# A two-layer hybrid decoder trunk on one core: the mixers' weight subtractions move from VectorE to GpSimd, and weights get four staging tiles instead of two

## The chip, the cores and the metric

The kernel runs on one core of a Trainium2 chip. The metric is the device time of one execution in microseconds (us); the median of three runs before the change is 2559.37 us (2557.65 to 2565.87).

Engine names are those of the profile: PE is TensorE's matmul, PEld its weight load, DVE is VectorE, ACT is ScalarE, POOL is GpSimd, SP is SyncE, which here only issues transfers. L94 is line 94 of the kernel.

## The reference

Input x is 1024 tokens by 1024 columns, fp32, and two layers are applied to it. Each layer is a mixer and an MLP, both with a norm ahead and a norm behind, added to x:

```python
h = rms_norm(x, g_pre_mix)
z = h @ w_in                      # 1024 x 2568: columns for three head groups
out_m = sigmoid(mo) * rms_norm(mlstm_chunkwise(...))       # 4 heads, chunks of 128
out_s = sliding_window_gqa(rope(sq), rope(sk), sv, sinks)  # 8 heads, window 128
out_d = rms_norm(differential_attention(rope(dq), rope(dk), dv, lam)) * (1 - lam_init)
x = x + rms_norm(concat([out_m, out_s, out_d]) @ w_out, g_post_mix)
h2 = rms_norm(x, g_pre_mlp)
x = x + rms_norm(square(relu(h2 @ w_up)) @ w_down, g_post_mlp)
```

All of it is fp32.

## The kernel before, in words

**Products in three parts.** Every large matmul is made from two parts of each operand. The high part (hi) is the fp32 value cast to the shorter type float32r, the low part (lo) is the value minus its high part. A product is then hi x hi + hi x lo + lo x hi, three matmuls in a row. For 128 rows of contraction the order is (weight hi, data hi), (weight hi, data lo), (weight lo, data hi), so a tile's first low part is read by its third matmul (in the combined projection of natural layout, by its second).

**Weights.** `load_w` (L103) brings a weight tile into SBUF in pieces of 512 columns (392 for the packing w_g). For each piece it takes a staging tile from the pool `raw` (tile rw), lets SP issue the transfer (L109), lets ACT cast it to the high part, and lets DVE subtract that from the staging tile, which gives the low part. Without a gain this is `split`:

```python
def split(hi, lo, src):
    nc.scalar.copy(hi, src)                              # L93
    nc.vector.tensor_sub(lo, src, hi.bitcast(F32))       # L94
```

The staging tile is free again when cast and subtraction are done; the next transfer into it waits for that on SP. `raw` has two tiles, 2 KB per partition each. The rest of the kernel uses `split` for activations too, so L93 and L94 appear with many tiles. The packings of w_in and the groups that load them are: w_t (13 tiles of 128x1024 per layer: differential q and k, sliding-window q and k, mLSTM q and k; `proj_tiles`, tile wt, matmuls L285), w_v (mLSTM values and output gate; `nat_group`, tile wv), and w_g (gates and the values of the other two; `p_g2`, tile wg). w_g of layer 0 has its own staging and does not go through `load_w`. w_out is loaded in `out_group` (tiles wo, or woh and wol). w_up (with a gain, L116 and L117, DVE) and w_down (tiles wdh and wdl) belong to the MLP.

**Order of the work.** The program is written as layer by layer: projections, differential attention (`e_diff`, four software-pipelined steps per pair of query blocks), the other projections, then sliding-window attention and mLSTM side by side, then the output projection in two groups of contraction tiles with the norms and transposes for the MLP, then the MLP in eight chunks of up and down. A scheduler with priorities orders the instructions on each engine when the program is built. `ahead(n)` raises the priority of what it encloses; weight loads have `ahead(1000)`. So the projections' matmuls fill PE while the attention waits, and weight transfers, casts and subtractions stand among the attention's instructions on SP, ACT and DVE. Each engine then runs its own list strictly in that order.

**What Pool did.** Pool computes the inverse roots of the norms (`rstd_of`, L153, tile rs, a power of -0.5), in differential attention a product with the softmax's reciprocal (L545, same tile), and some memsets (L672, L731 to L736). Nothing of the weights ran on it.

**Names in the profile.** rot, t and tab belong to the rotary embedding; d_rope, s_ropeq, s_ropek, m_qk, m_rows, mix_d and x_mid are DRAM tensors by which the stages hand on their results; ks, qs, kk and qq are attention operands read back from them. e is a tile of attention scores (L496 to L506), yc and z the mLSTM convolution (L683), h2T, hT and lT the transposed activations.

Of the kernel before, what the change touches and what calls it, by code (L numbers as in the profile page):

```python
# [10 lines left out]
F32 = mybir.dt.float32  # L11
# [6 lines left out]
P = 128  # L18
# [16 lines left out]
def hybrid_kernel(ctx: ExitStack, tc: tile.TileContext, x_in, w_t, w_g, w_v, w_out, w_up, w_down,  # L35
                  pb, cv, gains, g_mlp, rope_t, masks, out):
    nc = tc.nc
# [9 lines left out]
    def pool(tag, bufs, space=None):  # L47
        kw = {} if space is None else {"space": space}
        pools[tag] = ctx.enter_context(tc.tile_pool(name="p_" + tag, bufs=bufs, **kw))
# [6 lines left out]
    pool("at", 2)  # L56
    pool("pt", 2)
    pool("ev", 6)
    pool("raw", 2)
    pool("od", 3)  # L60
    pool("ys", 1)
    pool("mo", 1)
# [10 lines left out]
    def new(tag, shape, name, dt=F32):  # L73
        return pools[tag].tile(list(shape), dt, name=name, tag=tag)
# [10 lines left out]
    def PS(tag, name):  # L85
        return new(tag, (P, 512), name)

    def ahead(n):

        return tc.high_priority(offset=n) if n else nullcontext()  # L90
# [4 lines that stand above are left out]
# [5 lines left out]
        nc.scalar.copy(hi, raw)  # L100
        nc.vector.tensor_sub(lo, raw, hi.bitcast(F32))

    def load_w(hi, lo, src, step, gain=None):  # L103


        for c in range(0, hi.shape[1], step):
            with ahead(1000):
                r = new("raw", (P, step), "rw")
                nc.sync.dma_start(r, src[:, c:c + step])  # L109
            with ahead(1000):  # L110
                if gain is None:
                    split(hi[:, c:c + step], lo[:, c:c + step], r)
                    continue
                for j in range(step // P):
                    cs, rj, g = slice(c + j * P, c + j * P + P), r[:, j * P:j * P + P], gain[:, c // P + j:c // P + j + 1]
                    nc.scalar.activation(hi[:, cs], rj, AF.Copy, scale=g)  # L116
                    nc.vector.scalar_tensor_tensor(out=lo[:, cs], in0=rj, scalar=g, in1=hi[:, cs].bitcast(F32),  # L117
                                                   op0=ALU.mult, op1=ALU.subtract)
# [84 lines left out]
    for j in range(4):  # L203
        if j == 1:
            load_x(1)
        r = new("wd", (P, 2, 392), "wg0")
# [11 lines left out]
    for l in range(DEPTH):  # L218
# [37 lines left out]
        def proj_tiles(*groups):  # L256


            wts = []
            for idx, _, _, _, wtag in groups:  # L260
                for i in idx:
                    if wtag == "whl":
                        w = new("whl", (P, 2, 1024), "wt", F32R)
                        hi, lo = w[:, 0], w[:, 1]
                    else:
                        hi, lo = (new(wt_, (P, 1024), "wt", F32R) for wt_ in wtag)
                    load_w(hi, lo, w_t[l, i], 512)
                    wts.append((hi, lo))
            for half in range(2):
                wi = iter(wts)  # L270
                for idx, evac, tables, rtag, _ in groups:
                    if tables is not None:
                        with ahead(1000):
                            tab = new(rtag[1], (P, 2, 512), "tab")
                            nc.sync.dma_start(tab, rope_t[tables, :, :, half * 512:(half + 1) * 512])
                    qs = []
                    for i in idx:
                        hi, lo = next(wi)
                        q = PS("mm", "pt")
                        n = 0  # L280
                        for k in range(8):
                            kc = slice(k * P, (k + 1) * P)
                            for a, b in ((hi[:, kc], hT[half][:, :, kc]), (hi[:, kc], lT[half][:, :, kc]),
                                         (lo[:, kc], hT[half][:, :, kc])):
                                nc.tensor.matmul(q, lhsT=a, rhs=b, start=n == 0, stop=n == 23)  # L285
                                n += 1
                        qs.append(q)
                        if tables is None:
                            with ahead(1000):
                                evac(i, half, q)  # L290
                    if tables is not None:
                        with ahead(1000):
                            evac(half, qs, tab, rtag[0])
# [55 lines left out]
        def nat_mm(q, t, w_of, n):  # L349
            i = 0  # L350
            for k in range(8):
                lh = hT[t // 4][:, t % 4, k * P:(k + 1) * P]
                ll = lT[t // 4][:, t % 4, k * P:(k + 1) * P]
                wh, wl = w_of(k)
                for a, b in ((lh, wh), (lh, wl), (ll, wh)):
                    nc.tensor.matmul(q[:, 0:n], lhsT=a, rhs=b, start=i == 0, stop=i == 23)  # L356
                    i += 1
# [335 lines left out]
        def nat_group(idx, evac):  # L693
            wv = []
            for j in range(2):
                w = new("whl", (P, 2, 1024), "wv", F32R)
                load_w(w[:, 0], w[:, 1], w_v[l, idx, :, 1024 * j:1024 * j + 1024], 512)
                wv.append(w.rearrange("p s (k c) -> p s k c", k=4))
            for t in range(NT):
                q = PS("mm", "pn")  # L700
                nat_mm(q, t, lambda k: (wv[k // 4][:, 0, k % 4], wv[k // 4][:, 1, k % 4]), 256)
                with ahead(1000):
                    evac(t, q[:, 0:256])
# [118 lines left out]
        def out_group(k0, slots, first, fin):  # L822
            wo = []
            nk = 4
            for k in range(nk):
                if slots[k] == "whl":
                    w = new("whl", (P, 2, DM), "wo", F32R)
                    hi, lo = w[:, 0], w[:, 1]
                else:
                    hi = new(slots[k], (P, DM), "woh", F32R)  # L830
                    lo = new(slots[k], (P, DM), "wol", F32R)
                kt = mix_kt[k0 + k]
                load_w(hi, lo, w_out[l, kt * P:(kt + 1) * P, :], 512)
                wo.append((hi, lo))
            for t in range(NT):
                ts = slice(t * P, (t + 1) * P)
                mx = mxs[k0 // 4, t]
                with ahead(EARLY):
                    if k0 == 0:
                        load_split(mx[:, 0, 0:2], mx[:, 1, 0:2], mix_d[:, :, ts].rearrange("k p n -> p k n"))  # L840
                    else:
                        split(mx[:, 0, 2:4], mx[:, 1, 2:4], mst["out"][:, :, ts])
                for n in range(2):
                    q = PS("mm", "po")
                    i = 0
                    for k in range(nk):
                        for a, b in ((0, 0), (0, 1), (1, 0)):
                            nc.tensor.matmul(q, lhsT=mx[:, a, k], rhs=wo[k][b][:, n * 512:(n + 1) * 512],  # L848
                                             start=i == 0, stop=i == 3 * nk - 1)
                            i += 1  # L850
                    a = acc[t // 4][:, t % 4, n * 512:(n + 1) * 512]
                    with ahead(EARLY):
                        if first:
                            nc.scalar.copy(a, q)
                        else:
                            nc.vector.tensor_add(a, a, q)  # L856
                if fin is not None:
                    with ahead(1000):
                        fin(t)
# [75 lines left out]
        def p_g2():  # L935
            for k in range(8):
                if k < 4:
                    w = new("ws", (P, 2, 392), "wg", F32R)
                else:
                    if k % 2 == 0:  # L940
                        w2 = new("whl", (P, 2, 2, 392), "wg", F32R)
                    w = w2[:, k % 2]
                if l == 0:
                    split(w[:, 0], w[:, 1], wg0[k // 2][:, k % 2])
                else:
                    load_w(w[:, 0], w[:, 1], w_g[l, :, k, :], 392)
                wg.append(w)
            for t in range(NT):
                if l == 0 and t + 1 < NT:
                    first_norm(t + 1)  # L950
                g2(t)
            gating()
# [10 lines left out]
        def p_g1():  # L963
            nat_group(0, mv_evac)
            nat_group(1, mo_evac)
# [58 lines left out]
        for c in range(len(ffs)):  # L1024
# [4 lines left out]
            for f in range(nf):  # L1029
                w = new("whl", (P, 2, 1024), "wu", F32R)  # L1030
# [9 lines left out]
            for f in range(nf):  # L1040
                r0 = ffs[c][f] * P
                hi = new("wd", (P, DM), "wdh", F32R)
                lo = new("ws", (P, DM), "wdl", F32R)
# [60 lines left out]
            for j, (t, n) in enumerate(groups[4:]):  # L1104
                q = PS(ptag[j % 4], "pd")
                i = 0
                for f in range(nf):
                    i = down_mm(q, t, n, f, i)
# [93 lines left out]
```

## Time and profile before

| | |
|---|---|
| median of 3 runs | 2559.37 us |
| the profiled execution | 2563.38 us, its span 2561.6 us |
| mean granted TensorE clock | 0.972 |
| busy PE, DVE, ACT, Pool | 2397.5, 1457.8, 1076.1, 90.8 us |
| mixer of layer 0, MLP of layer 0 | about 0 to 593 us, 593 to 1250 us |
| mixer of layer 1, MLP of layer 1 | about 1250 to 1867 us, 1867 to 2561.6 us |

The span runs from the first to the last instruction of the program. Rows of groups read: line, engine, operation, output tile <- input tiles, shape, count, then busy us and mean ns of one, then the engine's idle time just before them and what ended most of it. The chain of waits is followed back from the last instruction: at each step to what released it, or else to the instruction before it on its engine. A piece of it that is a transfer means that nothing but that transfer was awaited there. "issue" is time in which an engine waited for nothing that the profile shows. Rows of waits read: who waited <- for whom: us in total, times, longest us.

### The profile page before, as it was taken

To read this page: it belongs to the slowest core of one execution; us is meant where nothing else is said; L and a number is where in the kernel's file an instruction comes from. 1 tells how busy PE (TensorE), PEld (TensorE's weight loads), DVE (VectorE), ACT (ScalarE), POOL (GpSimd) and SP (SyncE) were. 2 spreads that over 40 slices of the span, in tenths; PEclk is the share of its full clock that TensorE was granted. 3 is DMA by queue.
4 is the path that set the end of the run, shared out by engine and by line. 5 is a ranking of instruction groups with operands and counts; after the bars stand their busy time and mean duration, and the time that the engine had idled before them with its cause. 6 is when DMAs were issued, how large, how long until landed. Compare 5 with 4: busy or idle time off the path is not lost.

```text
span 2561.6 us, 32491 instructions
## 1 busy us (share of the span) xinstructions
PE 2397.5 (94%) x11556; PEld 1991.8 (78%) x11556; DVE 1457.8 (57%) x3604; ACT 1076.1 (42%) x2657; POOL 90.8 (4%) x174
## 2 busy tenths in 40 slices
PE   8888989889999999999999998878899999999998
PEld 7767867667888888888778777867678888888887
DVE  6676888775234434443675876867742344334436
ACT  4244777656313312331433645756553123213312
POOL 0000000010000000000000000000100000000000
PEclk9998999999999999999999989989999999999999
DMA  5444354333012101110442334433321112112204
GB/s 169 146 141 132 92 125 121 100 103 107 25 41 66 59 24 50 66 50 25 173 163 86 117 126 132 137 87 106 113 90 41 34 58 66 32 36 66 66 22 160
DMA packets 146002, 227.42 MB, mean 89 GB/s; under 512 B 22512, under 2 KB 60592, under 8 KB 145840
## 3 DMA queue, kind: packets, MB, share of 16 engines
q1 hardware_dynamic: 143680, 221.70, 28.1%
q10 hardware_dynamic: 2160, 3.65, 0.4%
q8 instruction: 91, 1.49, 0.2%
q14 instruction: 71, 0.58, 0.1%
HBM read 179.09 MB, written 46.20 MB: 88 GB/s over the span
## 4 chain that ended last, share of the span: by engine, by line
PE 73%; DMA 11%; DVE 7%; ACT 4%; issue 2%; POOL 1%; SPq 1%; DVEq 0%; POOLq 0%; ACTq 0%
PE pu L1012 26%; PE pd L1057 25%; PE pt L285 7%; PE po L848 2%; PE pg L356 2%; PE pn L356 2%; POOL rs L153 1%; DMA mb<-m_rows 1%; DMA qs<-d_rope 1%; PE pv L528 1%; DMA mix_d<-oo 1%; PE sp L493 1%; DMA mxl<-mix_d 1%; DMA rw<-in_w_t_dram 1%; PE ss L611 1%
## 5 line engine op out<-in xcount | busy, mean ns | idle before, releaser
L1012 PE MATMUL pu<-h2T,wu 128*128 128x512 f32 x3072 | 703.6, 390 | 0.1
L1012 PEld LDWEIGHTS pu<-h2T,wu 128*128 128x128 f32 x3072 | 577.4, 188 | 121.2 <-DVE h2T L94 1.1
L1057 PE MATMUL pd<-wdh,u 128*128 128x512 f32 x2048 | 635.2, 390 | 1.1 <-DVE acm L1068 1.1
L1057 PEld LDWEIGHTS pd<-wdh,u 128*128 128x128 f32 x2048 | 384.8, 188 | 81.1 <-DVE acm L1068 1.5
L1057 PE MATMUL pd<-wdl,u 128*128 128x512 f32 x1024 | 399.0, 390 | 0.0
L1068 DVE TENSOR_TENSOR acm<-acm,pd 128x512 f32<-128x512 f32 x224 | 153.1, 686 | 309.1 <-PE pd L1057 309.0
L1015 ACT ACTIVATE r<-pu 128x512 f32<-128x512 f32 x128 | 75.2, 588 | 537.9 <-PE pu L1012 537.9
L285 PE MATMUL pt<-hT,wt 128*128 128x512 f32 x832 | 287.2, 411 | 2.7 <-DVE lamp L228 1.5
L116 ACT ACTIVATE wu<-rw,gk 128x128 fp32r<-128x128 f32 x512 | 160.2, 390 | 184.7 <-PE pu L1012 132.3
L117 DVE SCALAR_TENSOR_TENSOR wu<-rw,gk,wu 128x128 fp32r<-128x128 f32 x512 | 154.2, 351 | 140.9 <-ACT wu L116 140.8
L1057 PEld LDWEIGHTS pd<-wdl,u 128*128 128x128 f32 x1024 | 192.6, 188 | 39.8
L1018 DVE TENSOR_TENSOR r<-r 128x512 f32<-128x512 f32 x128 | 88.4, 690 | 222.5 <-ACT u L1017 222.5
L285 PEld LDWEIGHTS pt<-hT,wt 128*128 128x128 f32 x832 | 160.5, 196 | 33.6 <-issue 2.3
L285 PE MATMUL pt<-lT,wt 128*128 128x512 f32 x416 | 170.2, 409 | 0.0
L153 POOL TENSOR_TENSOR rs<-ms,mhalf 128x1 f32<-128x1 f32 (+2 forms) x112 | 78.9, 709 | 2351.8 <-DVE ms L151 2283.2
L94 DVE TENSOR_TENSOR wdl<-rw,wdh 128x512 fp32r<-128x512 f32 x128 | 88.5, 692 | 105.1 <-ACT wdh L93 105.0
L848 PE MATMUL po<-woh,mxl 128*128 128x512 f32 x384 | 135.1, 410 | 10.4 <-DVE acc L856 7.8
L93 ACT CAST wdh<-rw 128x512 fp32r<-128x512 f32 x128 | 79.3, 620 | 129.2 <-DMA rw<-in_w_down_dram 129.2
L499 ACT ACTIVATE e<-e,nb 128x256 f32<-128x256 f32 (+7 forms) x128 | 99.4, 777 | 52.4 <-DVE nb L496 47.1
L493 PE MATMUL sp<-ks,qs 96*128 96x512 f32 (+2 forms) x192 | 74.0, 396 | 41.0 <-DMA qs<-d_rope 17.0
L356 PE MATMUL pn<-wv,hT 128*128 128x256 f32 x512 | 110.0, 296 | 0.2 <-ACT mv L707 0.2
L496 DVE CUSTOM_DVE_ANT_0 e<-sp,mdif 128x512 f32<-128x512 f32 (+3 forms) x128 | 74.5, 585 | 33.1 <-PE sp L493 24.0
(225 smaller groups left out, 3361.0 us busy)
## 6 DMA issues: line engine op xcount, KB each, us to landing
rw<-in_w_up_dram SPq DMA_DIRECT2D x128, 256.0 KB
rw<-in_w_down_dram SPq DMA_DIRECT2D x128, 256.0 KB
rw<-in_w_t_dram SPq DMA_DIRECT2D x52, 256.0 KB
tab<-in_rope_dram SPq DMA_DIRECT2D x20, 512.0 KB
xt<-in_x_dram SPq DMA_DIRECT2D x16, 512.0 KB
d_rope<-rot SPq DMA_DIRECT2D x32, 256.0 KB
s_ropeq<-rot SPq DMA_DIRECT2D x32, 256.0 KB
qq<-s_ropeq SPq DMA_DIRECT2D x16, 512.0 KB
```

What stands on the lines that cost most here:

```text
L94: nc.vector.tensor_sub(lo, src, hi.bitcast(F32))
L116: nc.scalar.activation(hi[:, cs], rj, AF.Copy, scale=g)
L117: nc.vector.scalar_tensor_tensor(out=lo[:, cs], in0=rj, scalar=g, in1=hi[:, cs].bitcast(F32), op0=ALU.mult, op1=ALU.subtract)
L153: nc.gpsimd.tensor_tensor(out=rs, in0=ms, in1=mhalf[:, 0:n], op=ALU.pow)
L285: nc.tensor.matmul(q, lhsT=a, rhs=b, start=n == 0, stop=n == 23)
L356: nc.tensor.matmul(q[:, 0:n], lhsT=a, rhs=b, start=i == 0, stop=i == 23)
L493: nc.tensor.matmul(sp[:, 0:w], lhsT=qs[0:96, m, (q % 4) * P:(q % 4 + 1) * P], rhs=ks[m][0:96, c0:c0 + w], start=True, stop=True)
L499: nc.scalar.activation(e[:, 0:L], e[:, 0:L], AF.Exp, bias=nb[:, nch - 1:nch], scale=-1.0, accum_out=den[:, m:m + 1])
L848: nc.tensor.matmul(q, lhsT=mx[:, a, k], rhs=wo[k][b][:, n * 512:(n + 1) * 512], start=i == 0, stop=i == 3 * nk - 1)
L1012: nc.tensor.matmul(q, lhsT=w[:, a, kc], rhs=h2[b + half][:, :, kc], start=n == 0, stop=n == 23)
L1057: nc.tensor.matmul(q, lhsT=U[f][a][:, t * P:(t + 1) * P], rhs=D[f][b][:, n * 512:(n + 1) * 512], start=i == 0, stop=i == 3 * nf - 1)
L1068: nc.vector.tensor_add(a, a, q)
```

## The change

The pool `raw` gets four tiles instead of two. `load_w` gets an argument that names the engine of the subtraction; for all packings of w_in and for w_out it is Pool, for w_down it stays DVE. w_up, which has a gain, keeps its path on ACT and DVE. The staging pool serves all of them.

```diff
-    pool("raw", 2)
+    pool("raw", 4)
...
-    def load_w(hi, lo, src, step, gain=None):
+    def load_w(hi, lo, src, step, gain=None, low=None):
...
                 if gain is None:
-                    split(hi[:, c:c + step], lo[:, c:c + step], r)
+                    nc.scalar.copy(hi[:, c:c + step], r)
+                    (low or nc.vector).tensor_sub(lo[:, c:c + step], r, hi[:, c:c + step].bitcast(F32))
                     continue
...
-                    load_w(hi, lo, w_t[l, i], 512)
+                    load_w(hi, lo, w_t[l, i], 512, low=nc.gpsimd)
...
-                load_w(w[:, 0], w[:, 1], w_v[l, idx, :, 1024 * j:1024 * j + 1024], 512)
+                load_w(w[:, 0], w[:, 1], w_v[l, idx, :, 1024 * j:1024 * j + 1024], 512, low=nc.gpsimd)
...
-                load_w(hi, lo, w_out[l, kt * P:(kt + 1) * P, :], 512)
+                load_w(hi, lo, w_out[l, kt * P:(kt + 1) * P, :], 512, low=nc.gpsimd)
...
-                    load_w(w[:, 0], w[:, 1], w_g[l, :, k, :], 392)
+                    load_w(w[:, 0], w[:, 1], w_g[l, :, k, :], 392, low=nc.gpsimd)
```

In the changed kernel the cast of a weight without a gain is L112 and its subtraction L113; every line behind them has a number that is one higher than before (rs is L154 and L546, the stores of rot are L319).

The scheduler makes new lists from this. On SP, at the start of layer 1's mixer, where the rotated q and k (rot) are stored to d_rope and read back as ks and qs, and the packing w_g is loaded into rw, the list before is:

```order
L318 DMA d_rope_11179<-rot 8x16x512 x2
L452 DMA ks<-d_rope_11179 32x2x512
L453 DMA ks<-d_rope_11179 64x2x512
L464 DMA qs<-d_rope_11178 64x2x512
L318 DMA d_rope_11178<-rot 8x16x512 x2
L465 DMA qs<-d_rope_11178 32x2x512
L318 DMA d_rope_11178<-rot 8x16x512 x2
L109 DMA rw<-in_w_g_dram 128x392 x3
L318 DMA d_rope_11179<-rot 8x16x512 x2
L109 DMA rw<-in_w_g_dram 128x392
L109 DMA rw<-in_w_t_dram 128x512
```

The same place on SP in the changed kernel:

```order
L276 DMA tab<-in_rope_dram 128x2x512
L319 DMA d_rope_11179<-rot 8x16x512 x2
L109 DMA rw<-in_w_g_dram 128x392 x2
L453 DMA ks<-d_rope_11179 32x2x512
L454 DMA ks<-d_rope_11179 64x2x512
L465 DMA qs<-d_rope_11178 64x2x512
L319 DMA d_rope_11178<-rot 8x16x512 x2
L466 DMA qs<-d_rope_11178 32x2x512
L319 DMA d_rope_11178<-rot 8x16x512 x2
L109 DMA rw<-in_w_t_dram 128x512 x4
```

Before, the last four of the eight w_g loads stand behind the first ks and qs loads and behind stores of rot. Now the last two stand ahead of them, the other six further up, and the next four loads of w_t come where three loads of w_g were.

On Pool, from the end of layer 0's differential attention to the start of layer 1 (rs of 128x4 is mLSTM's, rs of 128x1 that of the norms on whole rows, x32 of them in layer 0 and at its border), the list before is:

```order
L545 TENSOR_TENSOR rs<-rs,rd 128x2
L153 TENSOR_TENSOR rs<-ms,mhalf 128x4 x8
L153 TENSOR_TENSOR rs<-ms,mhalf 128x1 x32
L672 MEMSET z 128x3 x2
L153 TENSOR_TENSOR rs<-ms,mhalf 128x2
L545 TENSOR_TENSOR rs<-rs,rd 128x2
```

The same place on Pool in the changed kernel; mb is a buffer of the mLSTM, wo and wol are w_out, wt the first tiles of layer 1's w_t:

```order
L737 MEMSET mb_3889 128x2x2
L113 TENSOR_TENSOR wo<-rw,wo 128x512 x4
L113 TENSOR_TENSOR wol<-rw,woh 128x512 x4
L154 TENSOR_TENSOR rs<-ms,mhalf 128x4 x7
L113 TENSOR_TENSOR wol<-rw,woh 128x512 x4
L154 TENSOR_TENSOR rs<-ms,mhalf 128x4
L113 TENSOR_TENSOR wol<-rw,woh 128x512 x4
L154 TENSOR_TENSOR rs<-ms,mhalf 128x1 x16
L113 TENSOR_TENSOR wt<-rw,wt 128x512 x4
L154 TENSOR_TENSOR rs<-ms,mhalf 128x1 x11
L113 TENSOR_TENSOR wt<-rw,wt 128x512 x4
```

Before, nothing stood between these inverse roots. Now subtractions of weights stand ahead of the mLSTM's first rs, between its last ones, ahead of the norms of the output projection, and twice among the norms at the border of the layers. In differential attention they stand among the pairs of rs in the same way, mostly two at a time. In the whole list of Pool there are 108 of them, and at 29 places a run of them is followed by an rs. PE's own list in the mixers is reordered too, since the scheduler picks other projection matmuls between the attention's.

## The prediction

> **What bounds the kernel now.** I read the head of the page first, then the busy time by stage, then the chain of waits.
>
> ```profile
> span 2561.6 us, 32491 instructions
> PE 2397.5 (94%) x11556; PEld 1991.8 (78%) x11556; DVE 1457.8 (57%) x3604; ACT 1076.1 (42%) x2657; POOL 90.8 (4%) x174
> PE 73%; DMA 11%; DVE 7%; ACT 4%; issue 2%; POOL 1%; SPq 1%; DVEq 0%; POOLq 0%; ACTq 0%
> ```
>
> TensorE (PE) is busy for 94% of the span, and Pool is almost empty. The view of busy time by stretches, cut at the borders of the mixers and MLPs of the two layers, shows where the other 6% lie. A row is a stretch and its length, then busy us and instruction counts of PE, PEld, DVE, ACT and POOL, the granted clock, the DMA share and GB/s.
>
> ```profile
> 0.00:593.00 593.00, 511.72 (x2754) 427.28 (x2754) 429.26 (x1220) 336.12 (x867) 41.05 (x81) 0.95 0.43 126
> 593.00:1250.00 657.00, 655.78 (x2886) 542.13 (x2886) 271.90 (x536) 196.18 (x452) 0.00 (x0) 1.00 0.17 56
> 1250.00:1867.00 617.00, 543.00 (x2896) 454.17 (x2894) 455.88 (x1266) 341.11 (x878) 45.01 (x85) 0.94 0.40 120
> 1867.00:2561.60 694.60, 687.01 (x3026) 568.21 (x3024) 300.81 (x585) 202.69 (x463) 4.74 (x8) 1.00 0.18 60
> ```
>
> In the MLP stretches (rows 2 and 4) PE idles for 1.2 and 7.6 us. Nothing that concerns staging can be won there. In the mixer stretches (rows 1 and 3, together 1210 us) PE idles for 81.3 + 74.0 = 155.3 us, and DVE is busy for 429.3 + 455.9 = 885.2 us, 73%. So the change can act on those 155 us, and on them alone. The chain of waits says what ends last there; its summary by line and its long pieces:
>
> ```profile
> by line: PE pu L1012 25.6%; PE pd L1057 24.9%; PE pt L285 7.2%; PE po L848 2.5%; PE pg L356 2.4%; issue 2.0%; PE pn L356 1.9%; POOL rs L153 1.3%; DMA mb<-m_rows 1.3%; DMA qs<-d_rope 1.3%; PE pv L528 1.2%; DMA mix_d<-oo 1.2%; PE sp L493 1.2%
> ...
> 98.99 6.41 DMA rw<-in_w_t_dram
> ...
> 378.69 4.77 DMA rw<-in_w_out_dram
> ...
> 514.77 9.10 DMA rw<-in_w_up_dram
> ...
> 671.31 43.52 PE pu L1012 x192
> ...
> 1341.87 5.75 DMA rw<-in_w_g_dram
> ...
> 1785.73 7.95 DMA rw<-in_w_up_dram
> ```
>
> In the MLP the chain is unbroken PE (one piece of 43.52 us after another). In the mixers it hops between engines and transfers, and weight landings (tile rw) are among its pieces.
>
> **Part 1: four staging tiles instead of two.** A weight load is issued on SP when its rw buffer is free, that is when the low part two loads earlier has been subtracted. With four buffers it need only be four loads back, so the load of the next weight tile no longer follows the subtraction of this one. The order shows SP's loads standing earlier: in the stretch ahead of 1341.87 us above, the last w_g loads stood behind the ks and qs loads and several d_rope stores, and now stand ahead of them. What that is worth at most is PE's idle time inside these pieces of the chain, from the view by stretches with their borders:
>
> ```profile
> 98.99:105.40 6.41, 3.51 (x17) 2.60 (x15) 0.47 (x1) 0.00 (x0) 0.00 (x0) 0.94 0.64 205
> 378.69:383.46 4.77, 3.17 (x15) 1.62 (x13) 3.87 (x15) 4.73 (x14) 0.00 (x0) 1.00 0.91 267
> 514.77:523.87 9.10, 6.58 (x29) 5.07 (x27) 2.73 (x9) 0.42 (x1) 1.01 (x1) 1.00 0.37 101
> 1341.87:1347.62 5.75, 2.00 (x11) 1.62 (x9) 0.00 (x0) 0.00 (x0) 0.00 (x0) 0.95 0.50 166
> 1785.73:1793.68 7.95, 6.50 (x26) 4.72 (x26) 3.45 (x7) 2.38 (x5) 0.00 (x0) 1.00 0.36 104
> ```
>
> PE idles for 33.98 - 21.77 = 12.2 us in them. I take all of it, **-12.2 us**; the lower bound is nothing, if the next wait (mostly another transfer, as the chain's DMA share of 11% suggests) is just as late. In the MLP the deeper staging costs nothing, since PE's own work covers every load.
>
> **Part 2: subtractions leave DVE.** These are the groups of weight subtractions on DVE (count, then busy us, mean ns, idle time before and its cause):
>
> ```profile
> L94 DVE TENSOR_TENSOR wt<-rw,wt 128x512 fp32r<-128x512 f32 x52 | 34.9, 685 | 31.0 <-ACT wt L93 30.7
> L94 DVE TENSOR_TENSOR wol<-rw,woh 128x512 fp32r<-128x512 f32 x24 | 16.0, 687 | 3.2 <-ACT woh L93 2.1 <-PE ss L611 0.9
> L94 DVE TENSOR_TENSOR wv<-rw,wv 128x512 fp32r<-128x512 f32 x16 | 10.4, 684 | 0.0
> L94 DVE TENSOR_TENSOR wo<-rw,wo 128x512 fp32r<-128x512 f32 x8 | 5.4, 684 | 0.4 <-issue 0.3
> L94 DVE TENSOR_TENSOR wg<-rw,wg 128x392 fp32r<-128x392 f32 x8 | 4.4, 562 | 13.5 <-ACT wg L93 13.5
> ```
>
> That is 108 instructions and 34.9 + 16.0 + 10.4 + 5.4 + 4.4 = 71.1 us. DVE's part of the chain is 7% of 2561.6, 179 us, nearly all of it in the mixers, or 179/885.2 = 20% of DVE's busy time there. If the 71.1 us lie on the chain as often as the rest, they are worth 71.1 x 0.20 = **-14.3 us**. The rows also show 30.7 + 13.5 + 2.1 = 46.3 us in which DVE stood behind a copy on ACT that had not come; that blocking goes to Pool too. At the same 20% it would be another 9.3 us; I keep it for the low end only, since much of it is the same late landing as in part 1.
>
> **Part 3: what Pool takes for one.** No row shows a wide subtraction on Pool. The nearest:
>
> ```profile
> L545 POOL TENSOR_TENSOR rs<-rs,rd x32: 194/195/812, 145.2 to 1653.6; 128x2 f32<-128x2 f32 x32
> L734 POOL MEMSET mb<- 64x256 f32 x8 | 2.4, 305 | 0.3
> L736 POOL MEMSET mb<- 128x4 f32 x4 | 0.4, 109 | 0.2
> ```
>
> A two-input instruction with almost no elements takes 0.195 us (the middle one of min/median/max), and a written element costs (305 - 109)/252 = 0.78 ns, 0.40 us for 512. If both reads and the write run side by side, one takes 0.6 us; one after the other, 0.195 + 3 x 0.40 = 1.4 us. I take 1.2, nearer the upper end, because no row shows Pool overlapping them. 108 of them keep Pool busy for 130 us, 11% of the 1210 us, which it has. A page of the Trainium skill, GPSIMD Engine Reference, section 3.1, gives 4497 ns for 2048 fp32 elements of this kind; a quarter of that would be an estimate of 1.12 us, and the terms below would shrink by a few tenths.
>
> Each low part is ready 1.2 - 0.69 = 0.51 us later. A tile's third matmul reads it, but weights come ahead of use: of the 108, few were awaited.
>
> ```profile
> PEld sp L493 <- DVE wt L94: 4.9, 1, 4.9
> ```
>
> That is the longest such wait. I charge 8 cases, **+4 us** (bounds 0 and 108 x 0.51 = 55 us).
>
> **Part 4: Pool and DVE in each other's way.** The timeline shows, of Pool and then of DVE, one multiplication of two elements that took 0.64 instead of 0.195 us. It ended 0.06 us after a DVE instruction with both inputs in SBUF:
>
> ```profile
> 284.55 0.64 POOL L545 TENSOR_TENSOR rs<-rs,rd 128x2 f32<-128x2 f32 x1
> ```
> ```profile
> 283.85 1.28 DVE L506 SCALAR_TENSOR_TENSOR e<-e,r 128x1024 f32<-128x1024 f32 x1
> ```
>
> So DVE can hold Pool up. The reverse, Pool holding up DVE, no row shows, as no Pool instruction reads long. If it does, the victims are instructions like these:
>
> ```profile
> L506 DVE SCALAR_TENSOR_TENSOR e<-e,r 128x128 f32<-128x128 f32 (+3 forms) x64 | 51.9, 811 | 0.6
> L683 DVE SCALAR_TENSOR_TENSOR yc<-z,cvt,yc 128x512 f32<-128x512 f32 x48 | 35.8, 746 | 1.7 <-ACT yc L677 1.1 <-issue 0.2
> ```
>
> These two groups have 112 instructions; with the smaller groups of the kind I reckon about 300. Each meets a running subtraction in 11% of cases and waits half of 1.2 us: 300 x 0.11 x 0.6 = 20 us, at 20% on the chain **+4 us** (bounds 0, and the rival below). The Trainium skill, SBUF — State Buffer, section "Who interferes with whom", states that a DVE instruction with two SBUF inputs contends with a Pool instruction that reads SBUF, and that the second to issue fully blocks. The trace agrees for the one direction (0.64 us against 0.195).
>
> **Part 5: what is queued behind them on Pool.** Pool is in order, and its inverse roots (rs, L153, then a product, L545) now stand behind subtractions that themselves wait for ACT and a landing. In the order, a run of subtractions stands just ahead of an rs at 29 places. The first row here gives rs its mean:
>
> ```profile
> L153 POOL TENSOR_TENSOR rs<-ms,mhalf 128x1 f32<-128x1 f32 (+2 forms) x112 | 78.9, 709 | 2351.8 <-DVE ms L151 2283.2 <-DVE nb L618 30.2 <-DVE rd L502 25.3
> ```
>
> The chain gives rs 1.3%, 33.3 us, or 33.3/0.709 = 47 of 112: 42% of them are on the path. DVE waits for rs, and behind DVE the transposes on PE. If half a subtraction is in the way on average, 29 x 0.6 x 0.42 = **+7 us** (bounds 0, and the second rival).
>
> **The sum.** -12.2 - 14.3 + 4 + 4 + 7 = -11.5 us. The profiled execution took 2563.38 us (1.8 around its span), so 2551.9 of its kind. The median of the runs is 4.0 lower, 2559.37, so the forecast is **2548 us**.
>
> **The rivals.** First, the lock of part 4 works both ways and at full width: every subtraction keeps DVE from its two-input work for as long as DVE itself would have needed. Then -14.3 and its +4 vanish, and -12.2 + 4 + 7 = -1 leaves 2558 us: no change. For it: the 0.64 us row. Against it: DVE idles for 27% of the mixers, and an instruction with an input in PSUM has only one in SBUF. The rule of SBUF — State Buffer above is this rival's, read both ways; by it the time would be 2558.
>
> Second, slower: Pool's queue becomes the late one. Where two subtractions at 1.4 us stand ahead of each of the 29 rs, the push is 2.8 us, and 29 x 2.8 x 0.42 = 34 instead of 7; the sum is -12.2 - 14.3 + 4 + 4 + 34 = +15.5, or 2575 us. It decides once the mean push is over 18.5/(29 x 0.42) = 1.5 us. For it: the subtractions come in pairs, and the 46.3 us of DVE idling behind a late copy show that their inputs are not always there. Against it: most rs before had a long time free ahead of them (2351.8 us over 112), so many will find the pair done.
>
> **How the numbers follow.** A measurement of this kernel can tell about 0.3% from no change, 7.7 us: faster is below 2551.7, slower above 2567.1. The forecast has 0.60 (0.52 of it below 2551.7, 0.08 within), the lock 0.16 (within), the queue 0.24 (above). Low end: with the charges of parts 3 to 5 at zero and the 9.3 us of part 2, -35.8, or 2524. High end: the queue at its price, 2576. Outside lie some 0.05 below and 0.13 above.
>
> **What would show it.** Right: DVE's busy time in the mixers falls by 71 us; the five rw pieces leave the chain; PE's idle time in the mixers falls from 155 to about 144 us; Pool's group of subtractions has a mean near 1.2 us; the MLP pieces stay at 43.52 us. Wrong: DVE's groups L506 and yc get longer or wait for Pool (first rival); "DVE on" and "ACT acc" wait for POOL rs by tens of us, with Pool's rs standing behind a subtraction (second); or PE's idle time stays near 155 us though the rw pieces are gone, with other transfers in their place.

## The result, and the profile after

The changed kernel takes 2575.73 us (median of 4 runs, 2575.09 to 2579.17) against 2559.03 us (4 runs, 2557.65 to 2565.87). The ratio is 1.0063, with a 95% interval of 1.0043 to 1.0083: slower by some 17 us, where the forecast was 2548 us. The profiled execution took 2576.11 us, 1.8 us of it around the span.

The first lines of the page of the changed kernel:

```profile
span 2574.3 us, 32530 instructions
PE 2395.0 (93%) x11556; PEld 1982.3 (77%) x11556; DVE 1446.5 (56%) x3496; ACT 1069.6 (42%) x2657; POOL 238.6 (9%) x282
PE 22%; DMA 3%; DVE 2%; ACT 2%; POOL 1%; issue 1%; POOLq 0%; DVEq 0%; SPq 0%; ACTq 0%
```

108 instructions have left DVE (3604 before, 3496 now) and 108 have come to Pool (174, 282), as the diff says. But DVE's busy time fell by 1457.8 - 1446.5 = 11.3 us only, and the instructions that left had taken 71.1. So what stayed on DVE now takes 71.1 - 11.3 = 59.8 us longer. The third line sums up the chain of waits. Its shares make 31%, against 99% before: in this trace the chain reaches back only to about 1795 us, so its shares aren't comparable, and the next view has to serve.

Busy time by stretches. Each kernel is cut at the same matmuls: the last one of a layer's first group pu (up projection), and the last one of the first layer's last group pu. So rows 1 and 3 hold the mixers, and rows 2 and 4 the MLPs, row 4 with the end. Columns as in the prediction. Before, cut in this way:

```profile
0.00:627.40 627.40, 546.00 (x2897) 454.89 (x2898) 448.97 (x1259) 352.89 (x903) 41.05 (x81) 0.95 0.42 124
627.40:1236.68 609.28, 609.28 (x2690) 504.67 (x2688) 246.68 (x490) 175.70 (x408) 0.00 (x0) 1.00 0.15 50
1236.68:1900.82 664.14, 589.04 (x3091) 491.50 (x3090) 481.40 (x1312) 361.33 (x920) 45.01 (x85) 0.95 0.40 122
1900.82:2561.60 660.78, 653.19 (x2882) 540.72 (x2880) 280.79 (x546) 186.18 (x426) 4.74 (x8) 1.00 0.18 58
```

And after:

```profile
0.00:636.71 636.71, 544.98 (x2898) 454.64 (x2898) 451.31 (x1217) 355.49 (x911) 111.60 (x131) 0.96 0.41 124
636.71:1248.85 612.14, 611.23 (x2690) 503.96 (x2688) 243.09 (x481) 171.13 (x402) 2.54 (x2) 1.00 0.16 51
1248.85:1906.59 657.74, 583.53 (x3091) 483.74 (x3090) 476.49 (x1261) 361.91 (x926) 119.75 (x141) 0.96 0.40 121
1906.59:2574.30 667.71, 655.28 (x2882) 539.99 (x2880) 275.61 (x539) 181.03 (x418) 4.74 (x8) 1.00 0.17 56
```

The mixers went from 627.40 + 664.14 = 1291.5 to 636.71 + 657.74 = 1294.5 us. They hold all that the change was about, and gained nothing: PE's idle time in them, length minus busy, went from 156.5 to 165.9 us. The MLPs, which the forecast left untouched, went from 609.28 + 660.78 = 1270.1 to 612.14 + 667.71 = 1279.9 us. So 9.8 of the 12.7 us between the two spans lie in the MLPs. DVE in the mixers was busy for 930.4 us before and 927.8 now, although 42 + 51 instructions are missing there.

Which of DVE's instructions became longer shows in its groups (line, operation, operands and shapes, count, busy us, mean ns of one, idle time before). Before:

```profile
L504 DVE SCALAR_TENSOR_TENSOR r<-den,nlam,rd 128x1 f32<-128x1 f32 x64 | 13.5, 211 | 0.6
L618 DVE TENSOR_TENSOR nb<-nb,nsk 128x2 f32<-128x2 f32 x64 | 9.8, 153 | 0.2
L194 DVE SCALAR_TENSOR_TENSOR acm<-acm,rs,gh 128x512 f32<-128x512 f32 x32 | 22.2, 747 | 4.7 <-POOL rs L153 4.0 <-DMA x_new<-acm 0.6
L94 DVE TENSOR_TENSOR sb<-trs,sb 128x512 fp32r<-128x512 f32 x60 | 40.4, 683 | 4.2 <-ACT sb L93 3.8
```

After, with yc, whose row before (746 ns) stands in the prediction:

```profile
L684 DVE SCALAR_TENSOR_TENSOR yc<-z,cvt,yc 128x512 f32<-128x512 f32 x48 | 44.7, 932 | 2.5 <-ACT yc L678 2.0
L505 DVE SCALAR_TENSOR_TENSOR r<-den,nlam,rd 128x1 f32<-128x1 f32 x64 | 19.3, 302 | 0.7
L619 DVE TENSOR_TENSOR nb<-nb,nsk 128x2 f32<-128x2 f32 x64 | 14.7, 230 | 0.3
L195 DVE SCALAR_TENSOR_TENSOR acm<-acm,rs,gh 128x512 f32<-128x512 f32 x32 | 26.9, 895 | 5.4 <-POOL rs L154 5.4
L94 DVE TENSOR_TENSOR sb<-trs,sb 128x512 fp32r<-128x512 f32 x60 | 40.2, 680 | 2.4 <-ACT sb L93 2.0
```

The groups shown that read only SBUF tiles grew by a fifth to a half; sb, one of whose inputs (trs) lies in PSUM, stayed as it was. One place in the timeline shows what that is. On Pool (start us, duration us, then the instruction; two subtractions are drawn as one bar):

```profile
174.82 3.08 POOL L113 TENSOR_TENSOR wt<-rw,wt 128x512 fp32r<-128x512 f32 x2 [9.52 <-ACT wt L112]
```

DVE at the same time:

```profile
174.81 0.69 DVE L315 TENSOR_TENSOR rot<-rot,t 128x512 f32<-128x512 f32 x1
175.42 1.25 DVE L505 SCALAR_TENSOR_TENSOR r<-den,nlam,rd 128x1 f32<-128x1 f32 x1
176.59 0.68 DVE L316 TENSOR_TENSOR t<-pt,tab 128x512 f32<-128x512 f32 x1
177.19 1.79 DVE L507 SCALAR_TENSOR_TENSOR e<-e,r 128x1024 f32<-128x1024 f32 x1
```

And PE right after:

```profile
179.04 0.66 PE L521 MATMUL trd<-mk,e 128*128 128x128 f32 x4 [0.77 <-DVE e L507]
```

The rot that began 0.01 us before Pool keeps its 0.69 us. While Pool subtracts, an r of one element in each partition takes 1.25 us (mean before 0.21). The multiplication t next to it, which reads pt from PSUM, takes its usual 0.68. Then e takes 1.79 us, against 1.28 of its shape in the prediction's row, and PE stands for 0.77 us until e is there. In the waits of the whole run, the stops of PE's trd for DVE's e grew from 1 to 5 (0.4 to 3.5 us). These and PE's new waits for Pool and for ACT's r, in the changed kernel (engine and tile that wait, whom for, us in all, times, longest):

```profile
PE po L849 <- POOL wol L113: 4.5, 3, 1.7
PE trd L521 <- DVE e L507: 3.5, 5, 1.1
PE pt L286 <- POOL wt L113: 0.9, 2, 0.6
PE pn L357 <- POOL wv L113: 0.3, 1, 0.3
PE pu L1013 <- ACT r L1016: 5.3, 10, 1.0
```

The first, third and fourth are the late low parts. The last belongs to the MLP, and comes back below. Summed by the engine that PE waits for, the waits for DVE grew by 30.9 us and those for Pool by 5.7, while those for ACT fell by 22.5. The lists changed as well, so this sum alone doesn't say what made them grow.

### The profile page after: what moved, and what is told of

Its sections match the earlier page's. It is cut to its first block, busy times and chain, and to the rows that moved or that the text cites. A ratio compares the mean times of both kernels' runs of the same rounds, so it can differ in the third digit from the quotient of the medians.

```text
span 2574.3 us, 32530 instructions
## 1 busy us (share of the span) xinstructions
PE 2395.0 (93%) x11556; PEld 1982.3 (77%) x11556; DVE 1446.5 (56%) x3496; ACT 1069.6 (42%) x2657; POOL 238.6 (9%) x282
## 5 line engine op out<-in xcount | busy, mean ns | idle before, releaser
L154 POOL TENSOR_TENSOR rs<-ms,mhalf 128x1 f32<-128x1 f32 (+2 forms) x112 | 80.5, 720 | 1340.1 <-DVE ms L152 1315.3
L113 POOL TENSOR_TENSOR wt<-rw,wt 128x512 fp32r<-128x512 f32 x52 | 72.7, 1422 | 849.4 <-ACT wt L112 849.3
L113 DVE TENSOR_TENSOR wdl<-rw,wdh 128x512 fp32r<-128x512 f32 x128 | 87.1, 690 | 63.2 <-ACT wdh L112 61.9
L112 ACT CAST wdh<-rw 128x512 fp32r<-128x512 f32 x128 | 78.7, 616 | 85.4 <-DMA rw<-in_w_down_dram 85.3
```

The lines of the kernel that those rows point to most:

```text
L113: (low or nc.vector).tensor_sub(lo[:, c:c + step], r, hi[:, c:c + step].bitcast(F32))
L154: nc.gpsimd.tensor_tensor(out=rs, in0=ms, in1=mhalf[:, 0:n], op=ALU.pow)
```

## The experiments

Four theories were set against each other. **The lock** (L): while a Pool subtraction runs, DVE's instructions on SBUF tiles stand still, and those stops cost more than the relief brings. **The queue** (Q): Pool's inverse roots rs come late, since they stand behind subtractions. **The MLP theory** (M): four staging tiles let the loads of w_down, and ACT's casts of them, crowd what the MLP needs. **The order** (O): the new lists and the later low parts are what costs. Ratios are to the kernel before on the same chip, 95% intervals in brackets. Gains and losses in us come from these ratios or from the medians, which agree within some 2 us.

**The two halves of the change apart.** Staging alone is the kernel before with one line changed:

```
-    pool("raw", 2)
+    pool("raw", 4)
```

> Four staging tiles everywhere, all subtractions still on DVE. Theory M (four tiles put the MLP's w_down casts on ACT ahead of the evacuations of the up matmuls, which PE then awaits): the two MLP stretches are again 2.9 + 6.8 = about 10 us longer than before, and the mixers at best win the 12 us of the weight landings; ratio 0.998 to 1.006. Theory L (the loss is Pool's alone, through its lock with DVE or its queue): nothing on Pool has changed, so the MLP's up groups stay at 43.3 us and the time is 2547 to 2560 us, ratio 0.995 to 1.000.

Measured: 2544.25 us, 0.9947 [0.9930, 0.9964]. Its stretches:

```profile
0.00:623.40 623.40, 543.84 (x2897) 455.05 (x2898) 452.20 (x1267) 354.92 (x911) 43.39 (x81) 0.95 0.43 127
623.40:1235.80 612.40, 611.16 (x2689) 504.04 (x2689) 243.73 (x483) 171.42 (x402) 0.00 (x0) 1.00 0.16 51
1235.80:1878.50 642.70, 579.00 (x3092) 482.04 (x3091) 480.72 (x1317) 361.69 (x926) 45.30 (x85) 0.97 0.41 124
1878.50:2542.90 664.40, 655.25 (x2882) 540.07 (x2880) 276.32 (x539) 180.59 (x418) 4.75 (x8) 1.00 0.17 56
```

The mixers gain 1291.5 - 1266.1 = 25.4 us, twice M's most, and the MLPs lose 1276.8 - 1270.1 = 6.7, near M's 10. So the time lies below the ranges of both theories. Pool's subtractions alone are the changed kernel with the old staging:

```
-    pool("raw", 4)
+    pool("raw", 2)
```

> Subtractions of the mixers' weights on Pool, two staging tiles as before. Theory M: the MLP's up groups are back at 43.3 us each, so about 10 us of the changed kernel's loss are gone in the MLP; the mixers keep what Pool costs there, without the deeper staging that could win some back: ratio 1.000 to 1.006. Theory L: the time is as long as the changed kernel's or longer, ratio 1.006 or more, since all of the loss is Pool's.

Measured: 2593.77 us, 1.0142 [1.0124, 1.0161], and the whole loss lies in the mixers (1321.7 against 1291.5 us; the MLPs are at 1270.3). So the two halves pull in opposite directions, and the loss comes with Pool. DVE's busy time in it is 1439.4 us, a stretch of 1439.4 - (1457.8 - 71.1) = 52.7 us. The lists are new here too.

**The MLP with two staging tiles.** In the changed kernel (e3) and in the one with staging alone (e4), the mixers take their four tiles from two pools of two in turn, and the MLP's loads use only the first:

```
     pool("raw", 2)
+    pool("rax", 2)
...
+                turn[0] += not mlp
+                r = new("raw" if mlp or turn[0] % 2 else "rax", (P, step), "rw")
```

> As the changed kernel, but the MLP's loads use only two of the four staging tiles. Theory M: up groups at 43.3 us, about 10 us less than the changed kernel: 2564 to 2568 us, ratio 1.002 to 1.004. Theory L: no change against the changed kernel, 2575 us, ratio 1.006.

> Four staging tiles for the mixers, two for the MLP, all subtractions on DVE. Theory M: MLP as before, and the weight landings of the mixers may pay: 2547 to 2559 us, ratio 0.995 to 1.000, and faster than the kernel with four tiles everywhere by about 10 us. Theory L: the same as four tiles everywhere.

Measured: 2582.24 us, 1.0100 [1.0082, 1.0118], and 2547.68 us, 0.9963 [0.9948, 0.9978]. The MLPs came back to 1270.1 us in both, as M said, but the mixers rose by more than that: 1310.2 against 1294.5 us, and 1275.7 against 1266.1. M is right about the place and wrong about the net: its 1.002 to 1.004 for the first was missed. Where the mixers' loss comes from stays open: two pools in turn aren't one pool of four, and a mixer's first loads may start later behind an MLP with fewer tiles.

**One half of the MLP at a time.** With the same two pools, w_up takes four tiles and only w_down two, subtractions on DVE; then, apart from that, one pool of three for all:

```
-                load_w(hi, lo, w_down[l, r0:r0 + P, :], 512)
+                load_w(hi, lo, w_down[l, r0:r0 + P, :], 512, mlp=True)
```

> Four staging tiles for the mixers and w_up, two of them alone for w_down; all subtractions on DVE. Theory M (only the early casts of w_down hold up the evacuations in the MLP): the up groups are back at 43.3 us and the mixers keep what four tiles everywhere won there: 2537 us, ratio 0.992. If the gain of four tiles at the borders hangs on w_down's staging, or the lists come out otherwise: 0.995 to 0.997, no better than four tiles everywhere.

```
-    pool("raw", 2)
+    pool("raw", 3)
```

> Three staging tiles, all subtractions on DVE. If the gain of four tiles is the landings that no longer end a wait, three give a part of it: 0.996 to 0.999, with up groups in the MLP between 43.3 and 44 us. If it were chance in the lists, three could as well be slower than before.

Measured: 2547.66 us, 0.9966 [0.9952, 0.9979], and 2550.00 us, 0.9959 [0.9947, 0.9972]. The MLP rows of the first:

```profile
622.31:1231.59 609.28, 609.28 (x2689) 504.50 (x2688) 244.12 (x484) 173.03 (x402) 0.00 (x0) 1.00 0.15 51
...
1884.73:2545.50 660.77, 653.18 (x2882) 540.54 (x2880) 277.12 (x539) 182.76 (x418) 4.74 (x8) 1.00 0.16 56
```

Their lengths are those of the kernel before to 0.01 us, with w_up still at four tiles: the MLP's loss goes when w_down alone is back at two, and three tiles (MLPs 1270.1 us) don't cause it either. The 0.992 that M gave the first didn't come, since its mixers took 1275.5 us and not 1266.1. What four tiles do shows on ACT in the changed kernel, in a stretch of one up group, with PE's next stop:

```profile
1970.92 0.62 ACT L112 CAST wdh<-rw 128x512 fp32r<-128x512 f32 x1 [1.04 <-DMA rw<-in_w_down_dram]
1972.70 0.62 ACT L112 CAST wdh<-rw 128x512 fp32r<-128x512 f32 x1 [1.15 <-DMA rw<-in_w_down_dram]
1973.22 2.44 ACT L117 ACTIVATE wu<-rw,gk 128x128 fp32r<-128x128 f32 x8
...
1977.11 0.62 ACT L112 CAST wdh<-rw 128x512 fp32r<-128x512 f32 x1 [0.93 <-DMA rw<-in_w_down_dram]
1977.63 0.59 ACT L1016 ACTIVATE r<-pu 128x512 f32<-128x512 f32 x1
```
```profile
1978.27 3.92 PE L1013 MATMUL pu<-h2T,wu 128*128 128x512 f32 x16 [0.57 <-ACT r L1016]
```

Casts of w_down whose data hasn't landed stand one after another on ACT, the emptying of PE's buffer (r from pu) stands behind them, and PE stops for it. ACT's waiting for landings is not new as such: its casts of w_down waited for 129.2 us before, and for 85.3 in the changed kernel. New is that PE then waits for r: 5.3 us in 10 pieces here (the last row of waits above), 2.3 in 7 with staging alone, and none in the kernel before, in the variants of this and the last paragraph, or with Pool's subtractions alone. In the chain of waits of staging alone, landings of w_down make 3.5% of the span. PE's own waits are part of the 9.8 us only; how the rest comes about isn't shown. No variant beat staging alone: the intervals of e4, e8 and e11 overlap with its own.

**The lock by itself.** The kernel before, with one Pool subtraction added behind each of the 108 on DVE. It reads that piece's high part and a tile of ones, and nobody reads its result. By the traces, PE, ACT, DVE and SP otherwise run their instructions in the order of the kernel before (but for two transfers that ACT issues), here and in the next two runs.

```
+                    if extra:
+                        nc.gpsimd.tensor_sub(scr[:, 0:step], mones[:, 0:step], hi[:, c:c + step].bitcast(F32))
```

> The kernel before, which keeps its subtractions on DVE, with 108 further subtractions on Pool at the same places, waiting for the same casts and read by nobody; the lists of PE, ACT and SP are those of before, and DVE's but for one memset at the start. Theory L (Pool and DVE lock each other out): DVE's instructions with two SBUF inputs stretch by some 60 us in all, as in the changed kernel, and at a chain share of 20% the time grows by 12 us, ratio 1.003 to 1.007. Theory Q (Pool's queue delays rs): slower as well, with DVE and ACT waiting longer for rs. Theory O (the new lists and the later low parts are what cost): ratio 1.000, within 0.002, since neither is there.

The counter-test keeps the wait for the cast (one column read) and gives Pool about as much work, which only writes:

```
+                        nc.gpsimd.tensor_sub(scr[:, 0:1], mones[:, 0:1], hi[:, c:c + 1].bitcast(F32))
+                        for _ in range(1):
+                            nc.gpsimd.memset(scr, 0.0)
```

> As the extra subtractions, but what Pool does behind each cast is a one-column subtraction and a memset of 800 columns, about 0.9 us that write and do not read. Same lists on PE, ACT and SP. Theory L: no stretch of DVE's instructions, ratio 1.000, so the extra subtractions are slower than this by 12 us. Theory Q: as slow as the extra subtractions, or two thirds of it. Theory O: 1.000, like the extra subtractions.

Measured: 2615.36 us, 1.0234 [1.0213, 1.0256], for the subtractions; 2563.98 us, 1.0027 [1.0013, 1.0041], for the writes. The busy line, the group yc and the largest added group of the first:

```profile
PE 2414.3 (92%) x11556; PEld 1995.8 (76%) x11556; DVE 1539.0 (59%) x3605; ACT 1077.0 (41%) x2657; POOL 252.6 (10%) x282
L689 DVE SCALAR_TENSOR_TENSOR yc<-z,cvt,yc 128x512 f32<-128x512 f32 x48 | 40.0, 833 | 1.6 <-ACT yc L683 0.8 <-issue 0.4
L94 DVE TENSOR_TENSOR wt<-rw,wt 128x512 fp32r<-128x512 f32 x52 | 53.2, 1037 | 29.4 <-ACT wt L93 29.2
```

And of the second:

```profile
PE 2396.8 (94%) x11556; PEld 1989.5 (78%) x11556; DVE 1460.1 (57%) x3605; ACT 1075.8 (42%) x2657; POOL 219.4 (9%) x390
L691 DVE SCALAR_TENSOR_TENSOR yc<-z,cvt,yc 128x512 f32<-128x512 f32 x48 | 35.9, 747 | 1.7 <-ACT yc L685 1.1 <-issue 0.2
L120 POOL MEMSET scr<- 128x800 f32 x108 | 83.2, 770 | 6.2
```

Pool's work stands behind the same casts in both, and takes some 1.2 us a piece in the second (129 us in all) against 1.5 in the first (162). Where it reads SBUF, DVE grows by 1539.0 - 1457.8 = 81.2 us and the kernel by 60; where it only writes, DVE grows by 2.3 us and the kernel by 7 (3 to 10 by the interval). PE's waits for DVE, summed over the run, grow by 46.0 us in the first and by nothing in the second. So the lock is there, in the direction that no row of before showed; O can't be the cause of the 60 us, since neither new lists nor late low parts are there; and the queue is worth some 7 us. The sizes were missed: L had 1.003 to 1.007 for the subtractions and 1.000 for the writes. The Trainium skill, SBUF — State Buffer, section "Who interferes with whom", has DVE instructions with two SBUF inputs contend with a Pool instruction that reads SBUF, and not with one that only writes: these two runs agree (81.2 against 2.3 us), and so does the unchanged sb (683 and 680 ns).

In e5 more than half of the stretch, 46.8 us, falls on DVE's own subtractions, which follow the same cast (wt 1037 ns instead of 685). So the dose and the victims were varied. Half the columns:

```
-                        nc.gpsimd.tensor_sub(scr[:, 0:step], mones[:, 0:step], hi[:, c:c + step].bitcast(F32))
+                        nc.gpsimd.tensor_sub(scr[:, 0:step // 2], mones[:, 0:step // 2], hi[:, c:c + step // 2].bitcast(F32))
```

> The kernel with 108 extra subtractions on Pool, but each of them over half the columns (256 of 512, 196 of 392); the lists of PE, ACT and SP are again those of before. Theory L: the lock lasts half as long, so DVE's stretch falls from 81 us to 30 to 45 us, and the loss from 57 us to 20 to 35 us, ratio 1.008 to 1.014. Theory Q or anything that goes by the number of Pool's instructions and not by how long they read: the loss stays near 57 us, ratio 1.02.

Measured: 2580.20 us, 1.0075 [1.0062, 1.0088], with DVE at 1490.5 us: a stretch of 32.7 us instead of 81.2, and a loss of 19 us instead of 60. Both shrink, and by more than the half; the loss lies just below what L gave. Instructions on DVE that took over 0.1 us more than the median of their kind (operation, tiles and shape) before number 95 with an excess of 0.87 us each in e5, and 81 with 0.42 us each here: half the columns halve the stop. PE's waits for DVE grow by 11.1 us instead of 46.0.

**The mixers without their low parts, and the lock on top of that.** The mixers' low parts are left out: DVE subtracts one column, and the matmuls read the high part twice.

```
-                    split(hi[:, c:c + step], lo[:, c:c + step], r)
+                    n = 1 if cut else step
+                    nc.scalar.copy(hi[:, c:c + step], r)
+                    nc.vector.tensor_sub(lo[:, c:c + n], r[:, 0:n], hi[:, c:c + n].bitcast(F32))
...
-                    wts.append((hi, lo))
+                    wts.append((hi, hi))
...
```

> The mixers' low weight parts are left out: DVE subtracts one column of each piece instead of 512, and the matmuls read the high part in place of the low one. Two staging tiles, nothing on Pool. It shows what the relief of DVE is worth at its best. By the second step of the prediction: 71 us less on DVE at 20% is -14 us, ratio 0.994, and a little more as no low part is awaited. If DVE is not what the mixers wait for: 1.000, within 0.002.

The same with the 108 Pool subtractions of e5:

> The kernel without the mixers' low parts (DVE subtracts one column, the matmuls read the high part twice), with the 108 extra subtractions on Pool, which nobody reads. Lists of PE, ACT and SP as without the extra ones. It is the changed kernel's traffic, Pool subtracting and DVE not, without its late low parts and its new lists. Theory L: some 50 to 60 us of stretch on DVE's remaining two-input instructions, and 25 to 40 us more than without the extra subtractions: ratio to before 1.006 to 1.012. Theory O: as without them, 0.996, at most 0.999.

Measured: 2547.90 us, 0.9960 [0.9947, 0.9973], and 2597.29 us, 1.0158 [1.0143, 1.0173]. The busy lines of e7 and of e10, and e10's r:

```profile
PE 2393.5 (94%) x11556; PEld 1993.1 (78%) x11556; DVE 1410.4 (55%) x3604; ACT 1076.2 (42%) x2657; POOL 90.0 (4%) x174
```
```profile
PE 2403.8 (93%) x11556; PEld 1993.0 (77%) x11556; DVE 1480.8 (57%) x3605; ACT 1078.1 (42%) x2657; POOL 234.0 (9%) x282
L512 DVE SCALAR_TENSOR_TENSOR r<-den,nlam,rd 128x1 f32<-128x1 f32 x64 | 17.6, 275 | 0.6
```

From before to e7, 1457.8 - 1410.4 = 47.4 us off DVE brought 0.4%, 10 us (7 to 14 by the interval), or 0.21 us each if all of it is relief. That isn't shown. The scheduler made new lists for e7, and low parts are no longer awaited; PE's waits for DVE even grew by 7.7 us, while those for ACT fell by 25.0 and those for transfers grew by 11.0. So no run here prices the relief by itself.

From e7 to e10 the lists are the same (but for three of 11556 matmuls and a few transfers). DVE grew by 70.4 us and the ratio by 1.0158/0.9960 = 1.0199 (give or take 0.002, from the two intervals), some 50 us, more than L's 25 to 40. PE's waits for DVE grew by 40.6 us. With the 7 us of the queue taken off, that is 43/70.4 = 0.6 us of time for a us of stretch; e5 gives (60 - 7)/81.2 = 0.65 in the same way, and e9, with half the dose, (19 - 7)/32.7 = 0.37. So the price isn't one number. About half of the stretch in e10 still falls on DVE's own subtractions, now of one column: the 52 of wt went from 7.5 to 24.3 us, those of all packings by 34.

## Why the prediction was wrong

**Step that failed: part 4.** Of some 300 DVE instructions it said: "Each meets a running subtraction in 11% of cases and waits half of 1.2 us: 300 x 0.11 x 0.6 = 20 us, at 20% on the chain +4 us". Both the 20 us and the 20% were too small. The stretch is 59.8 us. In the trace of the changed kernel, 72 DVE instructions took over 0.1 us more than the median of their kind before, by 0.77 us on average (55 us in all), where the prediction had 33 of 0.6 us. The 11% took the subtractions as spread evenly, and the half of 1.2 us took victims as coming at any moment of one. The place at 174.82 us shows a pair back to back, with two victims in it, and r waits there for 1.25 - 0.21 = 1.04 us. An estimate of the cost, at the 0.37 of e9 to the 0.6 of e10, is +22 to +36 us instead of +4.

The 20% was DVE's average share of the chain. For stops it doesn't hold: e9 and e10 have about two to three times that. Why they cost more is argued only: among their victims are short steps (r, nb, e) that lie between PE's scores and PE's transposes, where there is little slack. PE's waits from e7 to e10 point that way, with trd for e going from 1.0 to 7.8 us and sp for nb from 4.5 to 8.6, but no run separates these steps from the rest.

**Rival 1 had the mechanism and not the price.** It let each subtraction keep DVE as long as DVE itself would have needed, 71.1 us in all, so that relief and lock cancel and 2558 us is left. 59.8 of the 71.1 us did come back as stops. If relief and stops cancelled, Pool's half alone would cost what parts 3 and 5 come to, some 13 us by what was measured; it cost 36, with whatever its new lists are worth in it. What stood against this rival, that DVE idles for 27% of the mixers, was true and didn't help.

**Rival 2 had the number and not the cause.** 2575 us is what was measured, but Pool's queue was to cost 34 us, and e6 has 7 for it. The waits for rs in the changed kernel agree: those of all instructions together rose from 47.2 to 53.5 us (staging alone has 58.4), and DVE's on for rs, the largest, rose from 13.0 us to

```profile
DVE on L548 <- POOL rs L546: 15.9, 21, 2.0
```

**Part 5** (+7) therefore stands as far as e6 can tell, whose pieces on Pool are a little shorter than the changed kernel's. **Part 3**: the sum of PE's three waits for Pool above is 4.5 + 0.9 + 0.3 = 5.7 us, against +4. The price of a subtraction was put at 1.2 us, and the groups show:

```profile
L113 POOL TENSOR_TENSOR wt<-rw,wt 128x512 fp32r<-128x512 f32 x52 | 72.7, 1422 | 849.4 <-ACT wt L112 849.3
L113 POOL TENSOR_TENSOR wol<-rw,woh 128x512 fp32r<-128x512 f32 x24 | 31.9, 1358 | 20.7 <-PE ss L612 10.6 <-ACT woh L112 10.1
```

That is 1.42 and 1.36 us, close to the upper end of 1.4, with Pool's stops behind DVE in it; the medians are 1.295 and 1.292 us. **Part 2** (-14.3) stays open: e7's 10 us would make -15 of it for 71.1 us, but e7 isn't relief alone, and its PE waited longer for DVE than before.

**Part 1** (-12.2) came close to the sum partly by luck. Staging alone brought -13 us. PE's idle time in its mixers fell from 156.5 to 143.3 us, so by 13.2, close to the term, and to the fall from 155 to 144 that the prediction named as a sign. Of the five landings, three are gone from its chain; those of w_g and w_up in layer 1 are still there, with 8.56 and 9.06 us. But its mixers are 25.4 us shorter: the other 12.2 lie in PE's busy time, with a granted clock of 0.97 instead of 0.95 in layer 1's mixer, and whether the clock made them isn't shown. Against that stand +6.7 in the MLPs (-18.7 together; the medians are 13 apart, since the profiled execution of before lies 4 us above the median of its own runs and 6 above that of the runs beside staging alone). The sentence "In the MLP the deeper staging costs nothing, since PE's own work covers every load" fell, a term put at nothing: it looked at PE's cover, and not at what the earlier casts stand in front of on ACT.

**The sum with measured terms**: staging -13, e7's gain taken whole -10, late low parts +6, queue +7 and stops +22 to +36 make +12 to +26 us for the change, measured +17; for Pool's half alone, -10 + 6 + 7 and 52.7 us of stops at 0.37 to 0.6 (19 to 32) make +22 to +35, measured +36. What the new lists are worth isn't known by itself. That the terms don't simply add is part of it: by the ratios, deeper staging took 1.0142 - 1.0063, 20 us, off the kernel with Pool's subtractions, and 14 off the one without.

## What to carry to other kernels

Before an elementwise instruction is moved to an idle engine, ask what it locks, not only how long it takes: here Pool's subtractions held up DVE for 59.8 us to free it of 71.1, and where the lists stayed the same, a us of stop cost 0.4 to 0.65 us of time. Pool's work that only writes (2.3 us of stretch for 108 fills) and DVE's subtractions with an input in PSUM (sb, 683 and 680 ns) showed little or none of it, so such are the candidates to stand side by side. And a change that goes two ways at once is worth its two halves apart: the staging alone is 0.5% faster than the kernel before, and the subtractions on Pool alone 1.4% slower.

## What was not expected of the hardware

A stop doesn't shrink with the victim: r, one element in each partition, took up to 1.25 us instead of 0.21, nearly as long as a whole subtraction on Pool (the shortest 1.26). Nor is the victim always a plain two-input instruction. These are the scalings of es by den, before and after:

```profile
L630 DVE TENSOR_SCALAR es<-es,den 128x256 f32<-128x256 f32 (+1 forms) x96 | 28.2, 337 | 0.0
```
```profile
L631 DVE TENSOR_SCALAR es<-es,den 128x256 f32<-128x256 f32 (+1 forms) x96 | 32.2, 378 | 0.2
```

Their second operand is a value for each partition, and they grew by 12%, the longest from 0.355 to 1.373 us. Pool's fills weren't quite free either: in e6 the longest sg from yc, with one tensor as input, took 0.742 us against 0.425 before. The estimate that the prediction worked out from the Trainium skill (GPSIMD Engine Reference, section 3.1), 1.12 us for a subtraction of 512 columns, is below the means of both groups, 1422 and 1358 ns, and below the shortest of them, 1266 and 1260 ns.
